# A down-projection as seven block products, with the operand sums on GpSimd

## The chip, the cores and the metric

The kernel runs on one core of one Trainium2 chip. The time is device microseconds of that core for one execution; the time before is the median of three runs. All lengths below are microseconds (us) unless ns is written. PE is the TensorE matmul engine and PEld its weight load, DVE is VectorE, ACT is ScalarE, POOL (Pool in the text) is GpSimd, SP issues DMAs, and a q behind a name is that engine's queue.

## The reference, cut to what matters

A transformer-like layer on 512 tokens with 1024 features each. It has a SwiGLU feed-forward stage, a mixer of two attention branches, and a second SwiGLU stage, and everything is float32:

```python
def swiglu(x, w1, w3, w2):
    return (jax.nn.silu(x @ w1) * (x @ w3)) @ w2

x = x + 0.5 * swiglu(rmsnorm(x, ffn1_norm[l]), ffn1_w1[l], ffn1_w3[l], ffn1_w2[l])
h = rmsnorm(x, mix_norm[l])
x = x + hybrid_mixer(h, w_in[l], b_gate[l], ...)
x = x + 0.5 * swiglu(rmsnorm(x, ffn2_norm[l]), ffn2_w1[l], ffn2_w3[l], ffn2_w2[l])
return rmsnorm(x, final_norm)
```

The inner width of a feed-forward stage is 2816, which is 22 chunks of 128. The change is in the last line but one, the second feed-forward stage (called "b" in the code): its down-projection is the product with `ffn2_w2`.

## The kernel before

Activations stand transposed: features on the 128 partitions, the 512 tokens along the free dimension. The state x is eight tiles of 128x512, `x0` to `x7` (listed as x_74 to x_81 in the order of instructions). To keep float32 accuracy with the fast matmul format, every operand is split into a high part H and a rest L, and a product is three matmuls (`mm3`, L260): H·H, H·L, L·H. A weight chunk of 128x1024 is loaded by DMA into a raw buffer, cast on ACT into `wh` (L247) and subtracted on DVE into `wl` (L248). There are four pairs of `wh` and `wl`, taken in turn, so a chunk can be cast once the chunk four places earlier has been used up on PE.

Stage b works in three groups of inner chunks, 0 to 8, 8 to 16 and 16 to 22. In each group:

- **Up.** Pairs of chunks f are computed by `strassen`: a 2x2 block product with seven block products in place of eight. Its steps are A11, S1, S2, A12, S3, S4, A22 (`STEPS`). S1 and S3 are sums of two blocks of weights, formed by a DMA that loads one block and a second DMA, issued by Pool, that adds the other on the way (L228, `wt`). S2 and S4 are sums formed on DVE (L246, `ws`). The operands on the other side are blocks of the activations; the PSUM banks called mm, X and Y collect the products, and `evict` moves them out after each step. One step is 24 matmuls of 128x256. The steps of consecutive pairs are interleaved.
- **Gate.** `evict` multiplies with the norm factor R, applies Silu, multiplies the two branches and keeps the result as H and L (`keep2`, L503 and L504) in the tiles `gg`.
- **Down.** `blocks` (L389) multiplies the group's 8 chunks with 64 blocks of `ffn2_w2`: 64 times three matmuls of 128x512, 192 in all, for the second group. Eight chunks of weights are loaded for it. Each of the eight output rows is then scaled by R and subtracted into x on DVE (L581, L582; the sign and the half are in the factor -0.5).

PE runs in an order written out by hand. The order on ACT, DVE, Pool and SP is set by a scheduler when the program is built. Each engine takes its instructions strictly in order, so an instruction that waits holds up everything behind it on its engine.

Of the kernel before, what the change touches and what calls it, by code (L numbers as in the profile page):

```python
# [30 lines left out]
GAP_S = 6  # L31
GAP_B = 1
LAG = 1
LAST = 2
WARM = 4
T = 512
# [30 lines left out]
def f32(t):  # L67
    return t.bitcast(F32)


class Layer:
# [53 lines left out]
    def turn_of(self, n):  # L125
        if self.kind[n] != "wt":
            return n
        s, f = self.order[n][0][2], self.order[n][1][0]
        if s == "q":
            return max(n - EARLY, self.index["swq", (0, "A11")] - 1)  # L130
        return n - (EARLIER if f >= GROUPS[s][1] else EARLY)
# [9 lines left out]
    def ffn_order(self, s):  # L141
        first, *ends = GROUPS[s]
        items, lo, n = [("w13" + s, i) for i in range(2 * first)], first, 0
        for hi in ends:
            items += [("sw" + s, at) for at in self.slots(range(lo, hi, 2), not lo)]
            nf = hi - (0 if n == 0 else lo)
# [35 lines left out]
    def offset(self, n):  # L182
        name, key = self.order[n][:2]
        if name[:2] == "sw":
            return 160 - 128 * (n % 2)
        if name == "w2b" and key >= (NF + GROUPS["b"][2]) // 2:
            return 96
        return 160 if name in ("w2a", "w2b", "wpa", "wpb", "wo") else 224
# [10 lines left out]
    def load(self, n):  # L199
# [16 lines left out]

        def part(q):
            if name[2] == "q" and f == FV:
                return self.a["wav0"][2 * int(q[1]) + int(q[2]) - 3].rearrange("p (a c) -> p a c", a=2)
# [11 lines left out]
    def prep(self):  # L231
# [5 lines left out]
        if both is None:  # L237
            return False
        name, key = self.order[n][:2]
        if n not in self.raws:  # L240
            self.load(n)
        raw, (H, L) = self.raws[n], both
        if name[:2] == "sw" and key[1] in ("S2", "S4"):
            a, b = (self.raws[self.index[name, (key[0], q)]] for q in (("S1", "A11") if key[1] == "S2" else ("S2", "A12")))
# [75 lines left out]
    def strassen(self, s, fs, evict):  # L320
        st, order = {}, self.slots(fs, s == "b" and not fs[0])
        end = self.used + len(order) - 1
        for f, step in order:
# [15 lines left out]
            evict(f, step, ps)  # L339
            yield  # L340

    def right(self, step, k):
# [139 lines left out]
    def ffn_run(self, s, gin, gnext, hooks, out=None, side={}):  # L482
# [33 lines left out]
        def folded(f):  # L516
            return out is not None and f >= ends[-2]

        def scale(t, a):
            t = t.rearrange("p (j n) -> p j n", j=2)  # L520
            nc.vector.tensor_mul(t, t, self.R[:, 256 * a:256 * a + 256].unsqueeze(1).to_broadcast([128, 2, 256]))

        def evict(f, step, ps):
# [15 lines left out]
            elif step == "S3":  # L539
                nc.vector.tensor_add(c2, ps, c2)  # L540
                if folded(f):
                    scale(lo, 0)
                    scale(c2, 1)
            elif step == "S4" and folded(f):
# [3 lines left out]
            elif step == "S4":  # L548
# [3 lines left out]
                nc.vector.tensor_mul(q, q, R)  # L552
                nc.scalar.activation(c1, c1, AF.Silu)
            else:
                if folded(f):
# [51 lines left out]
        for gi, hi in enumerate(ends):  # L607
# [8 lines left out]
            def done(d, ps, gi=gi, last=last):  # L616
                down(d, ps, last)
                if (gi, d) in side:
                    side[gi, d]()

            rows = [(list(g), lambda ps, d=d: done(d, ps)) for d in range(NK)]
            if last and out is not None:
# [752 lines left out]
def arrange(inp):  # L1375
# [9 lines left out]
    gqk = np.stack([p["q_norm"][0][half], p["k_norm"][0][half]]).reshape(1, 2, 2, 64)  # L1385
    out["gqk"] = np.broadcast_to(gqk, (128, 2, 2, 64))
    for s, n in (("a", 1), ("b", 2)):
        w1 = feat_chunks(p[f"ffn{n}_w1"][0])
# [5 lines left out]
        w2 = p[f"ffn{n}_w2"][0]  # L1394
        out["w2" + s] = np.concatenate([block_chunks(w2[128 * lo:128 * hi], LAST) for lo, hi in zip(ends, ends[1:])])
    w = p["w_in"][0]
# [32 lines left out]
```

## Time and profile before

| | us |
|---|---|
| median of 3 runs (lowest to highest) | 1240.81 (1240.38 to 1241.09) |
| profiled execution, its own time | 1240.7 |
| its span in the trace | 1238.9 |
| up part of the second group, stage b (1018.60 to 1094.87) | 76.27 |
| down part of it (1094.87 to 1138.41) | 43.54 |

The span is the stretch between the first and the last instruction in the trace; the profiled execution's time is 1.8 us longer. PE is busy for 99% of the span. A group of instructions is listed as line, engine, operation, out<-in; a timeline row is start, duration, engine, line, operation. PE rows overlap, since matmuls are pipelined: the pace of PE is read from the starts.

### The profile page before, as it was taken

How to read it: one execution, taken by the hardware profiler on the slowest of the kernel's cores; microseconds unless marked ns; L12 is line 12 of the kernel's file. 1: busy time of each engine (PE TensorE's matmuls, PEld its weight loads, DVE VectorE, ACT ScalarE, POOL GpSimd, SP SyncE). 2: the span in 40 equal slices, each digit the busy share in tenths (PEclk: the TensorE clock that was granted, in tenths of full speed). 3: DMA queues.
4: the chain of work that ended last, by engine and by line, in shares of the span. 5: the costliest groups of instructions: out<-in, count | busy, mean ns of one | idle time of the engine just before them, and what ended most of it. 6: DMA issues, size and time to landing. Idle time of an engine off the chain costs nothing.

```text
span 1238.9 us, 20489 instructions
## 1 busy us (share of the span) xinstructions
PE 1231.2 (99%) x8225; PEld 1115.5 (90%) x8225; DVE 906.2 (73%) x1348; ACT 605.9 (49%) x899; POOL 125.7 (10%) x131
## 2 busy tenths in 40 slices
PE   9999999999999999999999999999999999999998
PEld 7897999899899999988888888888899989988997
DVE  6985688468787887467746888865988757875874
ACT  7652355145465444454424446654665425532554
POOL 1111110000212110200001100000211001100001
PEclk9999999999999999999999999999999999999999
DMA  8783787241488972653232231267668537744222
GB/s 291 225 225 112 215 236 188 92 113 58 142 217 249 235 224 103 226 175 93 81 121 88 68 119 44 74 216 250 199 171 196 175 89 190 194 144 114 57 86 68
DMA packets 90206, 190.96 MB, mean 154 GB/s; under 512 B 12816, under 2 KB 18496, under 8 KB 90112
## 3 DMA queue, kind: packets, MB, share of 16 engines
q1 hardware_dynamic: 70896, 145.58, 34.7%
q0 software_dynamic: 18496, 43.54, 17.5%
q8 instruction: 64, 1.05, 0.3%
q10 hardware_dynamic: 720, 0.55, 0.1%
q14 instruction: 30, 0.25, 0.1%
HBM read 175.91 MB, written 17.38 MB: 156 GB/s over the span
## 4 chain that ended last, share of the span: by engine, by line
PE 98%; issue 1%; DMA 0%; SPq 0%; POOL 0%; POOLq 0%; ACT 0%; DVE 0%
PE mm L262 25%; PE mm L264 24%; PE mm L263 24%; PE Y L262 4%; PE Y L264 4%; PE Y L263 4%; PE X L262 2%; PE X L263 2%; PE X L264 2%; PE S L945 1%; PE mm L1023 1%; PE Tb L1159 1%; PE T L1034 1%; PE Sb L264 1%; PE Sb L263 1%
## 5 line engine op out<-in xcount | busy, mean ns | idle before, releaser
L247 ACT CAST wh<-wr 128x1024 fp32r<-128x1024 f32 x133 | 139.6, 1050 | 187.6 <-PE mm L263 129.5
L248 DVE TENSOR_TENSOR wl<-wr,wh 128x1024 fp32r<-128x1024 f32 x133 | 163.0, 1226 | 52.2 <-ACT wh L247 52.0
L262 PE MATMUL mm<-hH,wh 128*128 128x256 f32 (+1 forms) x560 | 179.5, 321 | 0.2 <-ACT wh L1300 0.2
L264 PE MATMUL mm<-hH,wl 128*128 128x256 f32 (+1 forms) x560 | 177.0, 316 | 0.0
L263 PE MATMUL mm<-hL,wh 128*128 128x256 f32 (+1 forms) x560 | 176.7, 316 | 0.0
L262 PE MATMUL mm<-gg,wh 128*128 128x512 f32 (+1 forms) x440 | 166.4, 378 | 0.0
L263 PE MATMUL mm<-gg,wh 128*128 128x512 f32 (+1 forms) x440 | 165.9, 377 | 0.0
L264 PE MATMUL mm<-gg,wl 128*128 128x512 f32 (+1 forms) x440 | 165.9, 377 | 0.0
L262 PEld LDWEIGHTS mm<-hH,wh 128*128 128x128 f32 x560 | 105.2, 188 | 9.2 <-ACT wh L1300 1.0
L264 PEld LDWEIGHTS mm<-hH,wl 128*128 128x128 f32 x560 | 105.1, 188 | 8.3 <-DVE wl L1301 0.4
L263 PEld LDWEIGHTS mm<-hL,wh 128*128 128x128 f32 x560 | 105.3, 188 | 7.4 <-DVE hL L411 0.2
L247 ACT CAST wh<-wa 128x1024 fp32r<-128x1024 f32 x54 | 56.8, 1051 | 94.6 <-PE mm L263 47.0
L262 PEld LDWEIGHTS mm<-gg,wh 128*128 128x128 f32 x440 | 82.6, 188 | 15.5 <-PE mm L264 0.2
L264 PEld LDWEIGHTS mm<-gg,wl 128*128 128x128 f32 x440 | 82.6, 188 | 15.4
L263 PEld LDWEIGHTS mm<-gg,wh 128*128 128x128 f32 x440 | 82.6, 188 | 15.0
L247 ACT CAST wh<-ws 128x1024 fp32r<-128x1024 f32 x54 | 56.8, 1052 | 71.3 <-PE mm L263 49.3
L247 ACT CAST wh<-wt 128x1024 fp32r<-128x1024 f32 x54 | 56.8, 1052 | 64.9 <-PE mm L263 41.6
L262 PE MATMUL mm<-TH,wh 128*128 128x256 f32 x320 | 88.4, 276 | 0.0
L263 PE MATMUL mm<-TL,wh 128*128 128x256 f32 x320 | 88.3, 276 | 0.0
L264 PE MATMUL mm<-TH,wl 128*128 128x256 f32 x320 | 88.3, 276 | 0.0
L248 DVE TENSOR_TENSOR wl<-wt,wh 128x1024 fp32r<-128x1024 f32 x54 | 65.9, 1223 | 28.6 <-ACT wh L247 27.9
L248 DVE TENSOR_TENSOR wl<-wa,wh 128x1024 fp32r<-128x1024 f32 x54 | 65.9, 1220 | 22.9 <-ACT wh L247 22.9
(284 smaller groups left out, 3198.5 us busy)
## 6 DMA issues: line engine op xcount, KB each, us to landing
wr<-in_w2a SPq DMA_DIRECT2D x22, 512.0 KB, 3.8
wt<-in_w13b SPq DMA_DIRECT2D x22, 512.0 KB, 3.8
wa<-in_w13b SPq DMA_DIRECT2D x22, 512.0 KB, 3.4
wt<-in_w13b POOLq DMA_DIRECT2D x22, 512.0 KB, 5.9
wr<-in_w2b SPq DMA_DIRECT2D x22, 512.0 KB, 3.7
wt<-in_w13a SPq DMA_DIRECT2D x18, 512.0 KB, 5.7
wt<-in_w13a POOLq DMA_DIRECT2D x18, 512.0 KB, 7.0
wa<-in_w13a SPq DMA_DIRECT2D x18, 512.0 KB, 6.5
```

The lines of the kernel that those rows point to most:

```text
L247: self.nc.scalar.copy(H, raw)
L248: self.nc.vector.tensor_sub(L, raw, f32(H))
L262: mm(out, lH, rH, start=start, stop=False, skip_group_check=more)
L263: mm(out, lH, rL, start=False, stop=False, skip_group_check=more)
L264: mm(out, lL, rH, start=False, stop=stop, skip_group_check=more)
L945: nc.tensor.matmul(*args, start=True, stop=True)
L1023: nc.tensor.matmul(oc, v, p, start=st, stop=sp)
L1034: nc.tensor.transpose(ps[:, 128 * b:128 * b + 128], P[h][:, c0 + 128 * b:c0 + 128 * b + 128], self.ident)
L1159: nc.tensor.transpose(pt[:, 128 * j:128 * j + 128], P[h, j][:, 128 * k:128 * k + 128], self.ident)
```

## The change

For the second group of stage b (`DOWN = (('b', 1),)`) the down-projection becomes a 2x2 block product too. The inner width of 1024 is split into two halves of 512, the 1024 outputs into two halves of 512 and the tokens into two halves of 256. The 512 outputs of a half are worked in two pieces of 256 (`half` 0 and 1). Each of the seven steps is done for both pieces: 14 products of 24 matmuls of 128x256, so 336 matmuls instead of 192 of 128x512. A11 is issued in two parts: three of its four chunks of the inner width for both pieces, then the fourth for both, which comes from the last pair of the up part.

Weights: `w2d` holds four blocks for each piece. S1 and S3 come by two DMAs as in the up part, S2 and S4 are sums on Pool (new L256). So 14 chunks are cast and split instead of 8, and 12 loads of 512 KB replace 8.

Activations: the gated result is kept as float32 in four blocks b0 to b3 (`G["t"]`, listed as T-2 and T-1) instead of being split. The seven operands are b0, b0-b1, -(b3+b0-b1), b2, b3-b1, b3 and (b3+b0-b1)-b2. The sums run on Pool in place (new L584, L586, L595, L600), and each operand is then cast on ACT and split on DVE (`divide`, new L575, L576, L578, L579) into two alternating buffers.

Scaling: R is applied in the up part's eviction for this group, the second scaling of each branch on Pool (new L628). Results: A11, S1 and S2 leave PSUM by an ACT copy and are added to x on Pool in pieces of 128x256 (new L613, L615). A12, S3, S4 and A22 are added to x on DVE straight from PSUM (new L619).

```diff
+DOWN = (('b', 1),)
...
+        if name[3:] == "d" and key[1] in ("S2", "S4"):
+            a, b = (self.raws[self.index[name, (key[0], q)]] for q in (("S1", "A11") if key[1] == "S2" else ("S2", "A12")))
+            self.nc.gpsimd.tensor_add(raw, a, b)
...
+    def down2(self, s, at, parts, evict):
+        name, st = "sw" + s + "d", {}
+
+        def products(half, step, cur, ops, ks=range(4)):
+            bank = {"S1": "Y", "S4": "Y", "A12": "X"}.get(step, "A")
+            fresh = step in ("A11", "S1", "A12") and 0 in ks
+            if fresh:
+                st[half, bank] = self.bank() if bank == "A" else self.aux(bank)
+            ps = st[half, bank]
+            for j in range(2):
+                for k in ks:
+                    w = [t[:, 512 * j + 128 * k:512 * j + 128 * k + 128] for t in cur]
+                    self.mm3(ps[:, 256 * j:256 * j + 256], *w, *(t[:, k] for t in ops), fresh and j == 0 and k == 0, k == 3,
+                             not (step in ("A11", "S1", "A12") and j == 0))
+            if 3 in ks:
+                evict(half, step, ps)
+
+        cur = [self.weights(name, ((at, half), "A11")) for half in range(2)]
+        ops = parts[0]()
+        for ks in (range(3), range(3, 4)):
+            for half in range(2):
+                products(half, "A11", cur[half], ops, ks)
+        ops = [parts[1]()]
+        for i, step in enumerate(STEPS[1:], 1):
+            ops.append(parts[i + 1]() if i < 6 else None)
+            for half in range(2):
+                products(half, step, self.weights(name, ((at, half), step)), ops[i - 1])
...
+        def divide(step, src, ks, sign=1.0):
+            H, L = (t[:, ks] for t in block(step))
+            if sign > 0:
+                nc.scalar.copy(H, src[:, ks])
+                nc.vector.tensor_sub(L, src[:, ks], f32(H))
+            else:
+                nc.scalar.activation(H, src[:, ks], AF.Copy, scale=sign)
+                nc.vector.scalar_tensor_tensor(L, src[:, ks], sign, f32(H), op0=ALU.mult, op1=ALU.subtract)
+
+        def first_parts(ks):
+            b = G["b"]
+            divide("A11", b[0], ks)
+            nc.gpsimd.tensor_sub(b[0][:, ks], b[0][:, ks], b[1][:, ks])
+            divide("S1", b[0], ks)
+            nc.gpsimd.tensor_add(b[0][:, ks], b[3][:, ks], b[0][:, ks])
...
+                if step in ("A11", "S1", "S2"):
+                    u = self.tmp.tile([128, T], F32, tag="t", name="u")
+                    nc.scalar.activation(u, ps, AF.Copy, scale=sign)
+                    for j, d in enumerate(rows):
+                        nc.gpsimd.tensor_add(self.x[d][:, cs], self.x[d][:, cs], u[:, 256 * j:256 * j + 256])
+                    return
+                for j, d in enumerate(rows):
+                    x = self.x[d][:, cs]
+                    self.pin = nc.vector.scalar_tensor_tensor(x, ps[:, 256 * j:256 * j + 256], sign, x, op0=ALU.mult, op1=ALU.add)
```

How the instructions stand at two places. The first is the passage from the up part of the second group to its down part. DVE, before (wl are the rests of weight chunks, c the gate's tiles, gg the split result, u and x the output):

```order
L552 TENSOR_TENSOR c_10998<-c_10998,R 128x1024
L248 TENSOR_TENSOR wl<-wr,wh 128x1024
L557 TENSOR_TENSOR c_10998<-mm,c_10998 128x512
L559 TENSOR_TENSOR c_10998<-c_10998,c_10999 128x512
L248 TENSOR_TENSOR wl<-wr,wh 128x1024
L504 TENSOR_TENSOR gg<-c_10998,gg 128x2x2x256
L248 TENSOR_TENSOR wl<-wr,wh 128x1024
L581 TENSOR_TENSOR u<-mm,R 128x512
```

DVE, after the change, at the same place:

```order
L628 TENSOR_TENSOR c_11010<-c_11010,R 128x512
L262 TENSOR_TENSOR wl<-wt,wh 128x1024
L668 TENSOR_TENSOR T-1_10706<-c_11010,c_11011 128x2x256
L669 TENSOR_TENSOR T-2_10705<-mm,c_11010 128x2x256
L262 TENSOR_TENSOR wl<-wt,wh 128x1024
L576 TENSOR_TENSOR gg<-T-2_10705,gg 128x256 x2
L262 TENSOR_TENSOR wl<-ws,wh 128x1024
L579 SCALAR_TENSOR_TENSOR gg<-T-2_10705,gg 128x1024
L262 TENSOR_TENSOR wl<-ws,wh 128x1024
L262 TENSOR_TENSOR wl<-wa,wh 128x1024 x2
L576 TENSOR_TENSOR gg<-T-2_10705,gg 128x1024
```

The two gate products (L668, L669) stand between weight splits, and the last pieces of the operands A11 and S1 (the two of 128x256), then those of S2 and A12, behind them. On Pool the before has only DMA issues here; with the change there stands:

```order
L256 TENSOR_TENSOR ws<-wt,wa 128x1024
L237 DMA wt<-in_w2d 128x1024
L584 TENSOR_TENSOR T-2_10705<-T-2_10705,T-1_10706 128x768
L628 TENSOR_TENSOR c_11010<-c_11010,R 128x512
L586 TENSOR_TENSOR T-2_10705<-T-1_10706,T-2_10705 128x768
L628 TENSOR_TENSOR c_11011<-c_11011,R 128x512
L584 TENSOR_TENSOR T-2_10705<-T-2_10705,T-1_10706 128x256
L595 TENSOR_TENSOR T-1_10706<-T-1_10706 128x1024
L586 TENSOR_TENSOR T-2_10705<-T-1_10706,T-2_10705 128x256
```

The sum for S3 (L595) was moved by the scheduler ahead of the last piece of the sum for S2 (L586). The second place is the middle of the down part, steps S2 to A22. Pool:

```order
L256 TENSOR_TENSOR ws<-ws,wa 128x1024
L615 TENSOR_TENSOR x_78<-x_78,u 128x256
L615 TENSOR_TENSOR x_79<-x_79,u 128x256
L256 TENSOR_TENSOR ws<-ws,wa 128x1024
L615 TENSOR_TENSOR x_80<-x_80,u 128x256
L615 TENSOR_TENSOR x_81<-x_81,u 128x256
L600 TENSOR_TENSOR T-2_10705<-T-2_10705 128x1024
L615 TENSOR_TENSOR x_74<-x_74,u 128x256
```

And DVE, from the split of S3's operand to that of A22's:

```order
L576 TENSOR_TENSOR gg<-T-1_10706,gg 128x1024
L619 SCALAR_TENSOR_TENSOR x_74<-X,x_74 128x256
L619 SCALAR_TENSOR_TENSOR x_75<-X,x_75 128x256
L262 TENSOR_TENSOR wl<-ws,wh 128x1024
L260 TENSOR_TENSOR ws<-wt,wa 128x1024
L619 SCALAR_TENSOR_TENSOR x_76<-X,x_76 128x256
L619 SCALAR_TENSOR_TENSOR x_77<-X,x_77 128x256
L262 TENSOR_TENSOR wl<-ws,wh 128x1024
L576 TENSOR_TENSOR gg<-T-1_10706,gg 128x1024
```

Four weight sums and splits, one weight sum for the next group (L260) and the results of A12 stand ahead of the operand of S4 (the last row). Before the change nothing of these was there but weight splits and the pairs L581 and L582.

More of the change, by code (lines that the diff above doesn't have):

```diff
@@ L145, in ffn_order @@
             items += [("sw" + s, at) for at in self.slots(range(lo, hi, 2), not lo)]
-            nf = hi - (0 if n == 0 else lo)
+            nf = hi - (0 if lo == first else lo)
+            if (s, ends.index(hi)) in DOWN:
+                at = DOWN.index((s, ends.index(hi)))
+                items += [("sw" + s + "d", ((at, half), step)) for step in STEPS for half in range(2)]
+                nf = 0
             items += [("w2" + s, n + i) for i in range(nf)]
@@ L516, in folded, with paired, block @@
         def folded(f):
-            return out is not None and f >= ends[-2]
-        def scale(t, a):
+            return out is not None and f >= ends[-2] or paired(f)
+        def paired(f):
+            return (s, sum(f >= e for e in ends)) in DOWN
+        G, ring = {}, {}
+        def block(step):
+            if step not in ring:
+                t = self.gtile(2 + STEPS.index(step) % 2)
+                ring[step] = [t[:, 1024 * c:1024 * c + 1024].rearrange("p (k n) -> p k n", k=4) for c in range(2)]
+            return ring[step]
@@ new lines, in evict2, with fn @@
+        def evict2(gi):
+            calls = iter(range(NK))
+            def fn(half, step, ps):
+                rows = range(2 * half, 2 * half + 2) if step in ("A11", "S2", "A12", "S4") else range(2 * half + 4, 2 * half + 6)
+                sign = -0.5 if rows[0] < 4 else 0.5
+                cs = slice(256, 512) if step in ("S1", "S2", "S3", "S4") else slice(0, 256)
+                if step in ("A11", "S1", "S2"):
[7 more added lines that the diff above has]
+                    self.pin = nc.vector.scalar_tensor_tensor(x, ps[:, 256 * j:256 * j + 256], sign, x, op0=ALU.mult, op1=ALU.add)
+                d = next(calls)
+                if (gi, d) in side:
+                    side[gi, d]()
+            return fn
@@ L1386, in arrange @@
     out["gqk"] = np.broadcast_to(gqk, (128, 2, 2, 64))
+    pairs = {}
     for s, n in (("a", 1), ("b", 2)):
@@ L1394, in arrange @@
         w2 = p[f"ffn{n}_w2"][0]
-        out["w2" + s] = np.concatenate([block_chunks(w2[128 * lo:128 * hi], LAST) for lo, hi in zip(ends, ends[1:])])
+        spans = list(zip(ends, ends[1:]))
+        out["w2" + s] = np.concatenate([block_chunks(w2[128 * lo:128 * hi], LAST) for i, (lo, hi) in enumerate(spans)
+                                        if (s, i) not in DOWN])
+        for at, (st, i) in enumerate(DOWN):
+            if st == s:
+                lo, hi = spans[i]
+                b = w2[128 * lo:128 * hi].reshape(4, 2, 128, 2, 2, 2, 128)
+                pairs[at] = b.transpose(4, 3, 1, 2, 5, 0, 6).reshape(2, 4, 128, 1024)
+    out["w2d"] = np.stack([pairs[at] for at in range(len(DOWN))])
     w = p["w_in"][0]
```

50 lines of the change are left out of this document (44 added, 6 removed).

## The prediction

> **What bounds the kernel now.** I read the page's busy times and its chain of waits first, then the stretches around the changed place.
>
> ```profile
> span 1238.9 us, 20489 instructions
> ...
> PE 1231.2 (99%) x8225; PEld 1115.5 (90%) x8225; DVE 906.2 (73%) x1348; ACT 605.9 (49%) x899; POOL 125.7 (10%) x131
> ...
> PE 98%; issue 1%; DMA 0%; SPq 0%; POOL 0%; POOLq 0%; ACT 0%; DVE 0%
> ```
>
> The chain is 98% PE: time changes one for one with what PE issues, as long as it does not wait. By stretch (columns: PE, PEld, DVE, ACT, Pool busy with counts, clock, DMA), the second group's up part and its down part:
>
> ```profile
> core 0: us, PE busy (x) PEld busy (x) DVE busy (x) ACT busy (x) POOL busy (x), PEclk, DMA share, GB/s
> 1018.60:1094.87 76.27, 76.27 (x674) 76.27 (x672) 62.35 (x62) 41.68 (x47) 8.44 (x7) 1.00 0.72 188
> 1094.87:1138.41 43.54, 43.54 (x194) 36.04 (x193) 23.10 (x27) 9.90 (x11) 1.20 (x1) 1.00 0.35 107
> ```
>
> PE never waits in either. DVE is 82% busy in the up part and 53% in the down part, ACT 55% and 23%, and Pool does nothing but issue DMAs. So the down part has much cover, and Pool looks free. The pace, from the starts of matmuls in time order:
>
> ```profile
> 1089.43 0.28 PE L262 MATMUL Y<-hH,wh 128*128 128x256 f32 x1
> ...
> 1092.15 0.28 PE L262 MATMUL mm<-TH,wh 128*128 128x256 f32 x1
> ...
> 1094.87 0.39 PE L262 MATMUL mm<-gg,wh 128*128 128x512 f32 x1
> ...
> 1138.41 0.28 PE L262 MATMUL mm<-hH,wh 128*128 128x256 f32 x1
> ...
> 1217.76 0.28 PE L263 MATMUL mm<-gg,wh 128*128 128x256 f32 x1
> ...
> 1221.64 0.28 PE L263 MATMUL mm<-gg,wh 128*128 128x256 f32 x1
> ```
>
> **Removed and added on PE.** Before: 192 matmuls in 43.54. After: 336 of 128x256, and 24 of those take 2.72 in a step of the up part, so 38.08: a gain of 5.46. The last two rows (33 matmuls in 3.88, 0.118 each) would make it 39.5 and the gain 4.0. I take 2.72, the same kind of step with the same weight loads. This gain holds only if 14 weight chunks and seven operands arrive in time.
>
> **What the operands cost.** The prices, from groups and single rows:
>
> ```profile
> L247 ACT CAST wh<-wr 128x1024 fp32r<-128x1024 f32 x133 | 139.6, 1050 | 187.6 <-PE mm L263 129.5
> L248 DVE TENSOR_TENSOR wl<-wr,wh 128x1024 fp32r<-128x1024 f32 x133 | 163.0, 1226 | 52.2 <-ACT wh L247 52.0
> ...
> L644 POOL TENSOR_TENSOR x<-x,R 128x256 f32<-128x256 f32 x2 | 1.4, 724 | 9.5 <-ACT R L454 9.5
> ...
> L228 POOL DMA_DIRECT2D wt<-in_w13b x22 | 26.6, 1232 | 395.5 <-DMA wt<-in_w13b 185.3 <-DVE u L581 93.7 <-DVE c L535 59.4
> ...
> 1085.65 0.68 DVE L557 TENSOR_TENSOR c<-mm,c 128x512 f32<-128x512 f32 x1
> ...
> 1214.30 0.42 DVE L578 SCALAR_TENSOR_TENSOR x<-mm,x 128x256 f32<-128x256 f32 x1 [1.43 <-PE mm L264]
> ```
>
> By these alone DVE has in the down part 14 splits of 1.23, about six operand splits of 1.23 and 16 evictions of 0.42, 31 of 38, and everything fits. But Pool's sums and DVE's splits do not run side by side. The places in the trace where both worked, DVE first:
>
> ```profile
> 868.49 0.42 DVE L894 TENSOR_TENSOR Traw<-Traw 128x256 f32<-128x256 f32 x1
> ...
> 873.50 1.25 DVE L894 TENSOR_TENSOR Traw<-Traw 128x256 f32<-128x256 f32 x1 [0.19 <-ACT Traw L890]
> ...
> 875.27 1.21 DVE L248 TENSOR_TENSOR wl<-wr,wh 128x1024 fp32r<-128x1024 f32 x1
> 876.40 0.47 DVE L411 SCALAR_TENSOR_TENSOR hL<-x,par,hH 128x256 fp32r<-128x256 f32 x1
> 876.80 0.67 DVE L1271 TENSOR_TENSOR x<-x,mm 128x512 f32<-128x512 f32 x1
> 877.40 1.88 DVE L248 TENSOR_TENSOR wl<-wr,wh 128x1024 fp32r<-128x1024 f32 x1
> 879.20 1.51 DVE L411 SCALAR_TENSOR_TENSOR hL<-x,par,hH 128x256 fp32r<-128x256 f32 x1
> ```
>
> ```profile
> 872.94 1.52 POOL L421 TENSOR_TENSOR acc<-acc,sq 128x512 f32<-128x512 f32 x1 [4.09 <-ACT sq L419]
> 874.41 2.44 POOL L228 DMA_DIRECT2D wt<-in_w13b  x2
> 876.57 1.61 POOL L421 TENSOR_TENSOR acc<-acc,sq 128x512 f32<-128x512 f32 x1
> 878.68 1.74 POOL L421 TENSOR_TENSOR acc<-acc,sq 128x512 f32<-128x512 f32 x1 [0.50 <-ACT sq L419]
> ...
> 1206.07 1.29 POOL L421 TENSOR_TENSOR acc<-acc,sq 128x512 f32<-128x512 f32 x1 [54.56 <-ACT sq L419]
> ```
>
> A Pool sum alone takes 1.29; beside DVE 1.52 to 1.74. The DVE instructions with two inputs in SBUF that start inside a Pool sum grow from 0.42 to 1.25, 1.21 to 1.88, 0.47 to 1.51. Taken off the recorded ends, each began 0.12 to 0.18 before the other's end: the two take turns, whoever asked first. An instruction with one input in PSUM (L1271, 0.67) is not held, nor is anything by a DMA issue (874.41). So a Pool sum of 512 holds DVE for 1.14 (from 878.07 to 879.13 the DVE split held Pool 1.06, from 879.13 to 880.24 Pool held DVE 1.11, and the one before 1.18). From the two sizes, 0.72 and 1.29, a quarter more of width is 0.57: holds of 0.57, 1.14, 1.71 and 2.28 for 256, 512, 768 and 1024. A DVE split holds Pool 1.07, one of 768 0.8, of 512 0.53, of 256 0.27.
>
> **The sum of the turns.** Zero is the end of the up part on PE. The last stretch without slack begins at -11.1: the second weight sum for S2 on Pool needs a buffer that DVE releases at -11.2 (its weight pair is free at -13.6, then 1.05 on ACT and 1.23 on DVE). From there to the split of A22's operand the order holds on Pool 5 sums of 1024, 2 of 768, 2 of 512 and 10 of 256: 11.4 + 3.4 + 2.3 + 5.7 = 22.8. On DVE 21 of 1024, 2 of 768, 3 of 512 and 2 of 256: 22.5 + 1.6 + 1.6 + 0.5 = 26.2. Together 49.0, so A22 cannot start before 37.9; without waits it would at 32.64 (12 of 14 products). At least 5.3 is lost of 5.46, with no pause in the turns. That is the bound from below. The bound from above is no waiting at all.
>
> **A walk through the order** with these holds, casts of 1.05 (0.35 for 256) and PE at 2.72 a product gives the pauses. The second weight sum ends at -8.8, a DMA issue follows to -7.5, the difference b0-b1 (three chunks) waits for its split at -6.85 and ends at -5.05. DVE's scaling is held until then; Pool's scale of the Silu branch runs to -2.2, DVE's split of S1's operand to -1.35, Pool's sum b0 to 0.4, the weight split of A11's second piece to 1.5, Pool's second scale to 2.6. Then in line on DVE: scaling 3.2, split 4.3, gate products 4.9 and 5.5, split 6.6, and the last chunk's split 6.95. PE wants it at 4.08: **a wait of 2.9**. The last chunk of S1 stands behind the sum for S3, moved ahead of it (7.7 to 9.95): **0.9**. S2 is on time (operand at 14.15, wanted at 14.67). Behind it four weight splits and four pieces of x alternate, and A12's operand comes at 20.2, **0.1** late. Pool's first sum for S4 follows (21.85 to 24.1), a split (25.2), a piece of x (25.75) and the operand of S3 at 26.85, wanted at 25.65: **1.2**. Then a piece of x to 27.4, DVE's two evictions of A12 to 27.6, and here Pool's second sum for S4 (27.55) and DVE's next split (27.6) ask within 0.1 of each other. If Pool is first: its sum to 29.8, split 30.9, piece 31.45, weight sum for the third group 32.55, evictions and the sum b2 to 35.5, split 36.6, piece 37.15, operand of S4 at 38.25, wanted at 32.3. If DVE is first, b2 falls behind that operand, which is there at 35.6: **6.0 or 3.3**. A22 then has its operand in time, and behind it the third group's first weights, four pairs ahead, are not late. Together 8.4 to 11.1, less 5.46: 3.0 to 5.6 slower. I take the middle, 4.3. On the profiled execution's 1240.7, which is 0.1 under the median, that is 1245.
>
> [...]
>
> The other edits change nothing on the path. Four more loads of 512 KB in the down part come at the up part's cadence, where DMA is busy 72% and PE doesn't wait. In the up part DVE loses a Silu scaling of 1024 and a split per pair and gains scalings; Pool's two scalings of 1.14 per pair take turns within DVE's 18% of slack, up to -11.
>
> **Rivals.**
> - *Clean gain.* Pool's turns are absorbed, since chunks can be cast three products (8.2) ahead and ACT is half idle. Then the gain is 4.0 to 5.46, less perhaps a wait of 1: 1235.3 to 1238. For it: PE has no wait in either part now. Against it: the 49.0 of turns in 43.7 (from -11.1 to 32.64). 17%.
> - *About nothing.* The turns interlock without pause, or Pool's pieces of x come late and out of the way: lost 5.3, gained 5.46, or with the last four pieces of x counted too (2.3) 2.1 slower: 1240.5 to 1243. 13%.
> - *Worse than the walk.* PE stands for 3.3 to 6.0 at S4 and comes back slower. The one slow stretch of this trace is its start:
>
> ```profile
> 4.83 0.79 PE L262 MATMUL mm<-hH,wh 128*128 128x512 f32 x1
> 5.42 0.48 PE L263 MATMUL mm<-hL,wh 128*128 128x512 f32 x1
> 5.74 0.41 PE L264 MATMUL mm<-hH,wl 128*128 128x512 f32 x1
> ...
> 7.15 0.39 PE L264 MATMUL mm<-hH,wl 128*128 128x512 f32 x1
> ```
>
> The first two come after 0.59 and 0.32 instead of 0.23, some 0.45 lost. Against that low price stands that PE had been at work before. At half pace for one product, 2.72 more, on the walk's upper end of 1246.3: 1249; the same after the wait at A11: 1252. 15%. [...]
> - *The change does not do what it says:* PE runs 128x256 at no better than 0.118: inside the first rival.
>
> **How the numbers follow.** The walk has 55%, with 1243.3 to 1249 as its own range. 0.2%, 2.5, is what a measurement here can tell from no change. Slower by more is the walk and the worse case, 70%; within it 13%; faster 17%. The range that leaves out some 10% of the clean gain below and some 8% above is 1236.5 to 1252.
>
> **What would show it.** Right: PE waits in the changed part, the first of 2 to 4 at A11's fourth chunk, the longest at S4, released by DVE's L576; DVE splits of 1.9 to 3.5 beside Pool sums of 1024; the down part 46 to 50 long. Wrong: a down part of 38 to 40 with splits of 1.23, or sums on Pool of 2.4 with unheld splits beside them. If instead PE waits for `wt` or `wr` DMAs, the loads were underrated. If the up part grows beyond 76.3, the scalings were.

## The result and the profile after

The changed kernel takes 1252.59 us (median of 4 runs, 1251.64 to 1253.83); the kernel before took 1240.95 beside it (4 runs). The ratio is 1.0095, with a 95% interval of 1.0078 to 1.0113: slower by 11.6, where the forecast was 4.3 slower and a range to 1252.0. The direction was right, the size was not. The profiled execution took 1253.83 and has a span of 1252.1.

The head of the page and its chain of waits, after the change. PE is still busy for 98% of a longer span, but DVE and Pool now stand in the chain:

```profile
span 1252.1 us, 20884 instructions
...
PE 94%; DVE 2%; issue 2%; POOL 1%; DMA 0%; ACT 0%; SPq 0%; POOLq 0%; DVEq 0%
```

By stretch (columns: PE, PEld, DVE, ACT, Pool busy with counts, clock, DMA, GB/s): the up part to its last matmul ahead of a pause, then that pause to the first matmul of the down part, then the down part:

```profile
1018.18:1092.30 74.12, 74.12 (x652) 74.00 (x650) 66.02 (x57) 38.50 (x47) 24.28 (x16) 1.00 0.69 178
1092.30:1099.53 7.23, 4.31 (x28) 4.14 (x27) 7.20 (x7) 2.17 (x4) 5.32 (x3) 0.82 0.42 132
1099.53:1151.74 52.21, 43.25 (x338) 42.66 (x337) 48.70 (x41) 23.40 (x28) 29.98 (x22) 0.89 0.56 145
```

The up part and the pause are 81.35 against 76.27, the down part is 52.21 against 43.54 (38.08 if nothing waited). Two of the three clocks are below 1.00. PE's waits in this stretch (us in total, times, longest), and the matmuls on both sides of each pause:

```profile
PE X L277 <- DVE gg L576: 6.7, 1, 6.7
PE mm L276 <- DVE c L647: 2.9, 1, 2.9
PE mm L277 <- DVE gg L576: 2.1, 1, 2.1
```

```profile
1092.30 0.28 PE L278 MATMUL Y<-hH,wl 128*128 128x256 f32 x1
1095.50 0.36 PE L276 MATMUL mm<-TH,wh 128*128 128x256 f32 x1 [2.92 <-DVE c L647]
...
1117.02 0.28 PE L276 MATMUL X<-gg,wh 128*128 128x256 f32 x1
...
1124.01 0.58 PE L277 MATMUL X<-gg,wh 128*128 128x256 f32 x1 [6.72 <-DVE gg L576]
...
1131.22 0.28 PE L276 MATMUL mm<-gg,wh 128*128 128x256 f32 x1
...
1133.60 0.38 PE L277 MATMUL mm<-gg,wh 128*128 128x256 f32 x1 [2.11 <-DVE gg L576]
```

The first pause lies in the up part, at the last step of its last pair; the second is at A12's operand, the third at S3's. None is at A11's fourth chunk or at S4.

**A ledger.** From the starts of all matmuls between 1018 and 1160 I count each gap above 0.3, less the 0.113 of a matmul at full pace (2.72 / 24), as a pause, and each gap of 0.14 to 0.3, less 0.113, as lost pace. After the change the pauses come to 12.8 and the lost pace to 5.4; less the 5.46 that PE gains this is 12.7, and the two spans differ by 13.2. The same count is made for the kernels below and comes within 0.9 of the spans. The parts are:

| | pause | lost pace behind it |
|---|---|---|
| up part, bank read by L647 (1092.30 to 1095.50) | 3.1 | 1.6 |
| S1, small (1106.47 to 1106.88) | 0.3 | |
| A12 (1117.02 to 1124.01, with 0.3 behind it) | 7.1 | 1.6 |
| S3 (1131.22 to 1133.60) | 2.3 | 1.6 |

The three stretches at half pace, 16 matmuls each, make 4.8 of the 5.4; the rest are single gaps, in some of which a record may be missing.

**The lost pace** is the granted clock. The stretch of matmuls at half pace that ends at 1100.38 is 3.41 long; in stretches of that length, counted from its end:

```profile
1093.55:1096.97 3.42, 1.47 (x12) 1.50 (x13) 3.42 (x3) 0.85 (x1) 2.52 (x3) 1.00 0.48 153
1096.97:1100.38 3.41, 3.41 (x18) 3.41 (x17) 3.38 (x4) 0.92 (x2) 1.91 (x1) 0.50 0.42 135
...
1127.68:1131.10 3.42, 3.42 (x31) 3.42 (x31) 3.42 (x2) 1.05 (x1) 3.42 (x4) 1.00 0.02 5
1131.10:1134.50 3.40, 1.29 (x11) 1.09 (x10) 3.40 (x5) 1.99 (x2) 0.23 (x1) 1.00 0.62 199
1134.50:1137.92 3.42, 3.42 (x19) 3.42 (x18) 3.38 (x5) 0.01 (x1) 1.50 (x2) 0.51 0.69 146
```

The two stretches in which PE works 1.47 of 3.42 and 1.29 of 3.40 are each followed by one whole stretch at 0.50 or 0.51, with 18 or 19 matmuls instead of 31. The stretch ahead of the first of them, 1090.14 to 1093.55, in which PE works 2.43 of 3.41, is followed by one at 1.00. The stretches at half pace behind the three pauses end on one grid of 3.41: at 1100.38, at 1127.7 (8 times 3.41 later) and at 1137.9 (11 times).

**What held DVE.** In the up part Pool's difference b0-b1 (L584) and its scaling (L628) hold two DVE instructions, and L647, which frees the bank that PE waits for, stands behind them. First Pool, then DVE:

```profile
1089.27 1.85 POOL L584 TENSOR_TENSOR T-2_10705<-T-2_10705,T-1_10706 128x768 f32<-128x768 f32 x1 [1.30 <-DVE gg L576]
...
1092.66 1.27 POOL L628 TENSOR_TENSOR c<-c,R 128x512 f32<-128x512 f32 x1 [1.54 <-ACT c L645]
```

```profile
1089.75 1.92 DVE L628 TENSOR_TENSOR c<-c,R 128x512 f32<-128x512 f32 x1
...
1092.73 2.02 DVE L576 TENSOR_TENSOR gg<-T-2_10705,gg 128x768 fp32r<-128x768 f32 x1
1094.67 0.68 DVE L647 TENSOR_TENSOR c<-mm,c 128x512 f32<-128x512 f32 x1
```

At A12 the turns that the forecast relied on are not kept. DVE, then Pool:

```profile
1111.15 1.76 DVE L262 TENSOR_TENSOR wl<-ws,wh 128x1024 fp32r<-128x1024 f32 x1
...
1114.51 4.80 DVE L262 TENSOR_TENSOR wl<-wa,wh 128x1024 fp32r<-128x1024 f32 x1
1119.24 4.72 DVE L576 TENSOR_TENSOR gg<-T-2_10705,gg 128x1024 fp32r<-128x1024 f32 x1
1123.88 6.86 DVE L262 TENSOR_TENSOR wl<-wt,wh 128x1024 fp32r<-128x1024 f32 x1
```

```profile
1115.15 0.73 POOL L615 TENSOR_TENSOR x<-x,u 128x256 f32<-128x256 f32 x1
1115.84 2.37 POOL L256 TENSOR_TENSOR ws<-ws,wa 128x1024 f32<-128x1024 f32 x1
1118.18 1.71 POOL L615 TENSOR_TENSOR x<-x,u 128x256 f32<-128x256 f32 x1
1119.86 0.71 POOL L615 TENSOR_TENSOR x<-x,u 128x256 f32<-128x256 f32 x1
1120.54 2.33 POOL L256 TENSOR_TENSOR ws<-ws,wa 128x1024 f32<-128x1024 f32 x1
```

The split at 1114.51 asks while a Pool sum runs that ends at 1115.18. Strict turns would start it there. Instead the next sum (0.73, its length alone) and a weight sum (2.37) go first, and only the third is held (1.71). The same happens to A12's operand (4.72), and at 1123.88 five sums pass a split. Against turns of 1.74 the two instructions ahead of A12 lose 3.1 and 3.0: most of the pause of 7.0.

### The profile page after: what moved, and what is told of

Its sections match the earlier page's. It is cut to its first block, busy times and chain, and to the rows that moved or that the text cites. A ratio compares the mean times of both kernels' runs of the same rounds, so it can differ in the third digit from the quotient of the medians.

```text
span 1252.1 us, 20884 instructions
## 1 busy us (share of the span) xinstructions
PE 1232.4 (98%) x8369; PEld 1123.3 (90%) x8369; DVE 943.0 (75%) x1363; ACT 619.0 (49%) x920; POOL 176.7 (14%) x165
## 4 chain that ended last, share of the span: by engine, by line
PE 94%; DVE 2%; issue 2%; POOL 1%; DMA 0%; ACT 0%; SPq 0%; POOLq 0%; DVEq 0%
PE mm L276 23%; PE mm L278 23%; PE mm L277 23%; PE Y L276 4%; PE Y L278 4%; PE Y L277 4%; PE X L276 2%; PE X L278 2%; PE X L277 2%; PE S L1068 1%; DVE wl L262 1%; PE mm L1146 1%; PE Tb L1282 1%; PE T L1157 1%; DVE gg L576 1%
## 5 line engine op out<-in xcount | busy, mean ns | idle before, releaser
L261 ACT CAST wh<-wr 128x1024 fp32r<-128x1024 f32 x127 | 133.3, 1050 | 173.8 <-PE mm L277 115.0
L262 DVE TENSOR_TENSOR wl<-wr,wh 128x1024 fp32r<-128x1024 f32 x127 | 159.2, 1253 | 50.9 <-ACT wh L261 50.8
L277 PE MATMUL mm<-gg,wh 128*128 128x512 f32 (+1 forms) x440 | 159.7, 363 | 2.1 <-DVE gg L576 2.1
L276 PE MATMUL mm<-gg,wh 128*128 128x512 f32 (+1 forms) x440 | 160.3, 364 | 0.0
L278 PE MATMUL mm<-gg,wl 128*128 128x512 f32 (+1 forms) x440 | 159.7, 363 | 0.0
L261 ACT CAST wh<-wa 128x1024 fp32r<-128x1024 f32 x58 | 60.9, 1051 | 89.5 <-PE Y L277 46.6
L261 ACT CAST wh<-ws 128x1024 fp32r<-128x1024 f32 x58 | 61.0, 1051 | 78.7 <-PE mm L277 43.7
L262 DVE TENSOR_TENSOR wl<-wt,wh 128x1024 fp32r<-128x1024 f32 x58 | 76.9, 1329 | 27.5 <-ACT wh L261 27.0
L278 PEld LDWEIGHTS mm<-gg,wl 128*128 128x128 f32 x440 | 83.5, 190 | 12.7
L262 DVE TENSOR_TENSOR wl<-wa,wh 128x1024 fp32r<-128x1024 f32 x58 | 79.4, 1370 | 19.1 <-ACT wh L261 19.1
L261 ACT CAST wh<-wt 128x1024 fp32r<-128x1024 f32 x58 | 60.9, 1051 | 63.1 <-PE mm L277 38.4
```

What stands on the lines that cost most here:

```text
L261: self.nc.scalar.copy(H, raw)
L262: self.nc.vector.tensor_sub(L, raw, f32(H))
L276: mm(out, lH, rH, start=start, stop=False, skip_group_check=more)
L277: mm(out, lH, rL, start=False, stop=False, skip_group_check=more)
L278: mm(out, lL, rH, start=False, stop=stop, skip_group_check=more)
```

## The experiments

The kernel before was timed beside all runs; its medians lie between 1240.66 and 1240.95. The ratios below are to it.

### Is it Pool's reads?

The first run takes the 12 sums of results on Pool away: A11, S1 and S2 are added to x by DVE, straight from PSUM.

```diff
-                if step in ("A11", "S1", "S2"):
-                    u = self.tmp.tile([128, T], F32, tag="t", name="u")
-                    nc.scalar.activation(u, ps, AF.Copy, scale=sign)
-                    for j, d in enumerate(rows):
-                        nc.gpsimd.tensor_add(self.x[d][:, cs], self.x[d][:, cs], u[:, 256 * j:256 * j + 256])
-                    return
...
+                if step in ("A11", "S1", "S2"):
+                    return
```

The loop between these lines, which adds A12, S3, S4 and A22 to x on DVE, now serves all steps.

> The results of A11, S1 and S2 are added to x on DVE straight from PSUM (one input in PSUM, 0.42 each), instead of an ACT copy and twelve Pool sums of 128x256; all else as in the change. Theory P (Pool's sums keep DVE's two-input instructions off SBUF, and do so for several sums in a row): the twelve sums are most of Pool's unbroken stretch of 1110 to 1131, so the wait of 6.9 at A12 falls to 2 or less and that of 2.3 at S3 with it; 1242 to 1247. Rival Q (Pool is only too slow, and DVE waits for its results): A12's operand b2 needs no sum, so its wait stays at 6 to 7; 1250 to 1253. Rival R (DVE has too much work): 12 instructions of 0.42 more on DVE, 1253 to 1257.

The second leaves every Pool sum out and lets Pool write the same output three times with memsets, which read nothing.

```diff
-            self.nc.gpsimd.tensor_add(raw, a, b)
+            self.fill(raw)
```

`fill` writes three memsets; all other Pool sums are replaced likewise, so the output is another one.

> Every sum that the change put on Pool is left out and three memsets of the same output stand in its place, so Pool is busy about as long and writes the same places, but reads nothing; the result is another one. Theory P: without reads DVE isn't held, the splits are back at 1.22, no wait at A12 or S3; 1235 to 1239. Rival Q (Pool's length and order alone are late): the waits stay; 1248 to 1254.

Measured: 1246.82 (1246.52 to 1247.34; ratio 1.0049, 1.0033 to 1.0066) and 1238.51 (1237.83 to 1238.99; ratio 0.9981, 0.9970 to 0.9991). Of PE's waits, in the first those in the up part and at A12, in the second the longest:

```profile
PE mm L276 <- DVE c L643: 2.9, 1, 2.9
...
PE X L277 <- DVE gg L576: 0.2, 1, 0.2
```

```profile
PE mm L277 <- DVE gg L583: 0.9, 1, 0.9
```

Without the 12 sums the wait at A12 is 0.2 instead of 6.7 and the one at S3 0.7 instead of 2.1, the one of 2.9 in the up part stays, and a new one of 1.9 stands at S2. With memsets in place of all sums the longest wait is 0.9 and the pauses come to 2.1; beside the memsets around the passage to the down part DVE's splits take 1.22. But this run does not tell reads from time at A12: a memset waits for no input, so the 36 memsets of x ran from 986.7 to 1021.5, some 90 or more ahead of their place, and behind 1114.4 Pool only issues DMAs. That a Pool sum holds DVE and a memset of the same width does not (3.36 and 1.21 beside 128x1024) is shown by the next kernel.

### The price of a turn

A measuring kernel of its own, which leaves the layer out: DVE differences of 128x1024 beside Pool sums of three widths, beside memsets, and with DVE's first input in PSUM; then matmuls with pauses of PE between them.

> A kernel of its own that leaves the layer out and only measures: 14 DVE differences of 128x1024 (two SBUF inputs) beside a full queue of Pool sums of 256, of 512 and of 1024, beside Pool sums that each wait for an ACT copy, beside Pool memsets, and 14 with one input in PSUM beside Pool sums of 1024; then matmuls after pauses of PE of about 1 to 6 us. Turn by turn (the prediction's rule): a DVE instruction takes 1.7 beside sums of 256, 2.3 beside 512, 3.4 beside 1024; Pool's sums grow by 1.07 each. If Pool keeps its place while its queue is full: single DVE instructions wait for 4 and more sums, others go two or three in a row. Memsets and the PSUM input: 1.14 to 1.22. PE: full pace after pauses up to about 3, half pace for some 3 us after longer ones, if the pause is the cause.

Rows of DVE, two in succession beside 256, one beside 1024, and one with its input in PSUM:

```profile
37.19 1.74 DVE L51 TENSOR_TENSOR owith<-xa,pb 128x1024 f32<-128x1024 f32 x1
38.86 1.74 DVE L51 TENSOR_TENSOR owith<-xa,pb 128x1024 f32<-128x1024 f32 x1
...
106.04 3.36 DVE L51 TENSOR_TENSOR owith<-xa,pb 128x1024 f32<-128x1024 f32 x1
...
198.30 1.22 DVE L51 TENSOR_TENSOR opsum<-wide,pb 128x1024 f32<-128x1024 f32 x1
```

Here the turns are strict, 1.74 for each DVE instruction beside 256, 2.28 beside 512, 3.36 beside 1024 (1.21 alone): each sum of a quarter more width adds 0.54, where the forecast had 0.57. Beside memsets and with an input in PSUM DVE takes 1.21 and 1.22. So the prices of the forecast were right, and the long rows of the changed kernel need something that this kernel does not have.

The matmuls show the clock again. Behind a pause of 2.7 (217.56 to 220.25) a stretch at about half pace follows at once; behind one of 3.3 PE runs 1.06 at full pace and then a stretch at half:

```profile
220.25:223.60 3.35, 3.35 (x16) 3.35 (x17) 0.00 (x0) 0.00 (x0) 0.00 (x0) 0.51 0.00 0
...
244.06:247.45 3.39, 3.39 (x18) 3.39 (x17) 0.00 (x0) 0.00 (x0) 0.00 (x0) 0.50 0.00 0
```

The ends, 223.6 and 247.45, are 7 times 3.41 apart, though the pauses differ (2.7 and 3.3). The expectation had full pace after pauses of up to about 3, a limit that no run shows; that failed, as the half pace behind 2.7 says.

### Is it the clock?

14 matmuls on R ahead of A12, which are overwritten, keep PE busy while it waits for A12's operand; nothing else is changed.

```diff
+            for _ in range({("A12", 0): 14}.get((step, half), 0) if fresh else 0):
+                self.nc.tensor.matmul(ps[:, :256], self.R[:, :128], self.R[:, :256], start=True, stop=True)
```

> Fourteen matmuls of R with itself (128x256, float32, into the bank that A12 overwrites) are put ahead of A12, into the wait of 6.9; their product is used by nothing. Theory: the half pace behind the pauses (0.21 per matmul, 3.4 us lost in the down part) comes of PE's standing still; kept busy, it loses 1.4 to 3.4 less: 1249 to 1251. Rival: the pace falls for another reason (power, the operands): 1252 to 1254, no gain.

Measured: 1253.51 (1252.92 to 1254.84; ratio 1.0104, 1.0089 to 1.0119), no gain: the time of the rival, though not for its reason. The stretch behind A12, and the one behind S3:

```profile
1123.04:1126.00 2.96, 2.96 (x25) 2.96 (x26) 2.96 (x1) 0.02 (x1) 2.96 (x3) 1.00 0.49 176
...
1132.65:1137.00 4.35, 4.35 (x20) 4.35 (x21) 4.32 (x7) 0.00 (x0) 1.89 (x2) 0.50 0.71 169
```

The half pace behind A12 is gone, so it did come of PE's standing still. But S3's operand comes no earlier for it (16.6 after the start of the pause at A12 in both kernels): PE waits 3.9 there instead of 2.3, and pays the clock behind that, for more than one stretch of 3.41 (4.35 at 0.50). The 1.6 that the dummies saved at A12 is waited at S3. Where a row of late operands sets the time, a faster PE between two of them is worth nothing.

### Moving the sums to DVE, part by part

Scalings alone (L628), results and scalings, these and the weight sums (L256), and all, with the operand sums (L584, L586, L595, L600); then the operand sums alone, and all but the results. The results go to DVE as in the first run; each other part is the same edit at its line:

```diff
-            self.nc.gpsimd.tensor_add(raw, a, b)
+            self.nc.vector.tensor_add(raw, a, b)
```

Where these expectations and the later ones speak of a port, the rows show that DVE and Pool take turns (1.74 beside sums of 256) and that memsets have no part in it (1.21), and no more than that.

> One part of the change alone is undone: the two scalings per pair of the gate that ran on Pool (L628) run on DVE again; all other Pool sums stay. Theory P (DVE stands behind Pool's sums at the shared port): PE's pause of 3.2 in the up part, at the bank that L647 reads, came from DVE instructions held by these scalings, each 1.14. With them gone the pause is under 1, the half pace after it (2.0) goes too, and the time is 5.2 below the changed kernel's 1252.6: 1246 to 1249, with the pause of 7.0 at A12 still there. Rival Q (the pause comes from Pool's weight sum for S2 and from b0-b1, not from the scalings): the pause stays between 2 and 4 and the time at 1251 to 1254.

> Results of A11, S1 and S2 on DVE from PSUM (as in x_on_dve) and also the scalings on DVE. Pool keeps four weight sums and six operand sums. Theory P: the up part's pause of 3.1 and the half pace after it go, 5 less than x_on_dve's 1246.8: 1240.5 to 1243.5, what is left being pauses of 1 to 2 in S2 and S3. Rival Q (another sum sets the up part's pause): 1246 to 1248. Rival D (DVE's own work becomes the bound: two scalings of 0.67 per pair and 12 evictions of 0.42 are 7 more on DVE): pauses released by DVE grow in the down part, 1244 to 1247 with no pause in the up part.

> As the one before, and the weight sums for S2 and S4 on DVE too. Pool keeps only the six operand sums. DVE gets four sums of 1.23 (4.9) and loses four holds of 2.28 (9.1). Theory P: 1237 to 1240, with pauses of under 2 in all. Rival D (DVE's work is the bound): about the same as with the weight sums on Pool, 1240.5 to 1243.5.

> Every sum of the change on DVE, Pool only issues DMAs. Theory P: no hold is left; DVE has 21 splits of 1.23, 5 sums of 1.23, some 7 of smaller size and 24 evictions of 0.42 in the last 49 before A22, some 45, so it fits only just, and pauses of 1 to 3 stay: 1236 to 1240, the gain of 5.5 less the pauses. Rival D (DVE's own time is what the change costs wherever the sums run): 1241 to 1246.

> Only the operand sums (L584, L586, L595, L600) move to DVE; scalings, weight sums and x sums stay on Pool. Adding up what each part was worth when it was moved (6.9 for the operand sums, as the last part moved): 1245 to 1247. If the parts are not to be added because one row of Pool sums is as good as another at passing DVE over: the pause at A12 stays at 3 to 7 and the time at 1249 to 1253.

> Pool keeps only the 12 sums per half-group of results into x (24 of 256, 0.57 of hold each) with their ACT copies; scalings, weight sums and operand sums run on DVE. Against every sum on DVE (1237.4) DVE saves the evictions of A11, S1 and S2, 12 of 0.42, 5.0, and is held 12 times 0.57, 6.8. Theory A (strict turns): within 2 of 1237.4, 1236 to 1240. Theory B (Pool's row of sums passes DVE over for several sums at a time): single DVE instructions of 3 to 7, a PE pause of 2 to 5 with half pace after it, 1240 to 1245.

(There are 12 sums of 256 for the results, not 24.) Measured, with the ledger's two sums:

| on DVE | median | ratio, 95% interval | pauses | lost pace |
|---|---|---|---|---|
| nothing (the change) | 1252.59 | 1.0095 (1.0078 to 1.0113) | 12.8 | 5.4 |
| results | 1246.82 | 1.0049 (1.0033 to 1.0066) | 7.1 | 4.1 |
| scalings | 1252.90 | 1.0096 (1.0081 to 1.0112) | 12.8 | 4.7 |
| results, scalings | 1248.45 | 1.0062 (1.0049 to 1.0074) | 8.9 | 3.4 |
| results, scalings, weight sums | 1244.28 | 1.0028 (1.0017 to 1.0039) | 5.7 | 2.3 |
| operand sums | 1247.55 | 1.0055 (1.0040 to 1.0070) | 7.7 | 4.0 |
| all but the results | 1243.86 | 1.0023 (1.0013 to 1.0033) | 6.0 | 3.1 |
| all | 1237.37 | 0.9973 (0.9963 to 0.9982) | 1.2 | 0.4 |

With all sums on DVE the change is 0.27% faster than the kernel before: 3.4 of the 5.46 arrive, and one wait of 0.8 is left. This version beats both kernels, though DVE has the most instructions there (1393 against 1363 in the changed kernel): its busy time even falls, from 943.0 to 928.3, since nothing holds it (splits of 1.21 and 1.22 at the passage to the down part).

The expectation for the scalings was wrong. The pause in the up part did fall from 3.1 to 1.3, so they made the larger half of it, but DVE's own work then comes later into the down part: PE waits 3.6 at S1 and 4.3 at S2, no longer at A12, and the time stays. Also with the results already on DVE, moving the scalings costs 1.6. The parts do not add up: the results are worth 5.8 as the first part to go and 6.5 as the last, the operand sums 5.0 and 6.9, the scalings nothing or less. What a sum costs depends on what it stands in front of. Of the other expectations here, those for all sums on DVE (theory P) and for all but the results (theory B) held; results with scalings (1248.45) and these with the weight sums (1244.28) came out above all their windows, and the operand sums alone (1247.55) between their two.

### When does Pool pass DVE over?

A second measuring kernel: the sums in place, mixed widths, DVE starting at other moments, and DMA issues of Pool directly ahead of its sums.

> A measuring kernel of its own that leaves the layer out: 12 to 14 DVE differences of 128x1024 beside a row of Pool sums, in sections: DVE's first start shifted by 0.2 to 0.7 (four sections), Pool's 24 sums of 256 in place, a mix of 256, 256 and 1024 in place, two accumulating DMA issues or two plain ones directly ahead of the 24 sums with DVE starting at once or 1.4 later, and a mix in which each two sums wait for a fresh ACT copy, without and with the accumulating issues ahead. Theory A (strict turns everywhere, DVE was not ready in the changed kernel for another reason): every DVE instruction that meets 256-wide sums takes 1.74, and none waits for more than one sum. Theory M (an issue of a DMA on Pool leaves its sums overlapping, so that the port does not come free between them): waits over several sums, 2.4 and more, in the sections with an issue ahead and in no other. Theory I (sums in place keep the port): in the in-place sections too. Theory O (it depends on when DVE asks): in some of the shifted sections, with nothing else changed.

In the four shifted sections, with sums in place, with the mix, and with sums that wait for ACT, the turns are strict throughout (1.74, and 3.35 beside 1024). Behind two DMA issues they are not (the issue, the first DVE row that meets the sums, and Pool's 24 sums as one row):

```profile
195.56 1.19 POOL L90 DMA_DIRECT2D acc<-in_x  x1
196.13 16.86 POOL L83 TENSOR_TENSOR x<-x,u 128x256 f32<-128x256 f32 x24
```

```profile
195.91 18.17 DVE L46 TENSOR_TENSOR odma<-xa,pb 128x1024 f32<-128x1024 f32 x1
```

One DVE instruction waits for the whole row of 24 sums, 18.17 instead of 1.74; 17.55 and 17.40 behind plain loads. With the accumulating issues and DVE asking later it is passed over in no place, and in the mix behind an issue only by the sums of 1024, 4.04 instead of 3.35. So in this kernel no DVE instruction is passed over without an issue ahead, as theory M said, and an issue does not always suffice. A third kernel asks what ends it.

> A second measuring kernel that leaves the layer out: what ends the row in which Pool's sums pass DVE over after Pool has issued DMAs. Sections, each with 8 DVE differences of 128x1024: two plain issues, then 16 sums of 256 with a Pool memset of 64, 256 or 512 between them (the memset does not use the port); one memset of 512 only between the issues and the sums; a wait of Pool for eight ACT copies there; the issues in the middle of a row of 18; accumulating issues with DVE asking 0.7 to 2.8 later; sums of 1024 behind issues. If Pool's sums pass DVE over because the next one asks before the last one has let go everywhere (the start of one overlaps the end of the one before), a memset between them lets DVE in: no DVE instruction above 2 in the sections with memsets between, and above 5 in the section with none. If it is a state that an issue leaves for a length of time (the descriptors are still being worked on), the section with the wait shows turns of 1.74 and the memsets change nothing. In the middle of a row: 1.74 ahead of the issues, passed over behind them.

A row of 16 sums directly behind two plain issues passes DVE over (12.19); one memset of 0.54 in between restores the turns (1.74). Each time DVE, then Pool:

```profile
300.36 12.19 DVE L46 TENSOR_TENSOR oagain<-xa,pb 128x1024 f32<-128x1024 f32 x1
...
85.18 1.74 DVE L46 TENSOR_TENSOR oonce<-xa,pb 128x1024 f32<-128x1024 f32 x1
```

```profile
300.55 10.91 POOL L83 TENSOR_TENSOR x<-x,u 128x256 f32<-128x256 f32 x16
...
84.16 0.54 POOL L92 MEMSET gap<- 128x512 f32 x1
```

Memsets of 256 or 512 between the sums restore the turns too, those of 64 do not (13.53), and a wait of Pool for ACT does. With the issues in the middle of a row the turns hold ahead of them, and behind them DVE waits 9.4 for the twelve sums that are left. When DVE asks later behind accumulating issues, two of four sections are passed over (12.17, 12.12) and two are not: it depends on the moment as well. Behind issues, rows of six sums of 1024 pass DVE over too (14.99 and 15.77). Neither theory fits whole: by the first the memsets of 64 should have let DVE in, by the second no memset should have, and no row shows the descriptors that it speaks of.

### Does passing over make the loss?

Every sum stays on Pool; behind each of the down part (not behind the scalings) comes a memset on a tile that is free there, and behind the accumulating loads of stage b from its second group on one of 128x512 (the first run has both, the second only the latter, the third both on the version with only the results on Pool).

```diff
+    def gap(self, inst, w):
+        with self.tc.issue_after(inst.ins):
+            self.nc.gpsimd.memset(self.acc[:, :w], 0.0)
...
-            self.nc.gpsimd.tensor_add(raw, a, b)
+            self.gap(self.nc.gpsimd.tensor_add(raw, a, b), 256)
```

> The changed kernel with a Pool memset of 128x256 on a free tile behind each Pool sum of the down part, and one of 128x512 behind each of Pool's accumulating loads. Nothing is left out and no sum is moved from Pool; Pool's row gets about 5 longer. In the measuring kernel such memsets gave the port to DVE after each sum. Theory B (being passed over by several sums in a row makes the pause of 7.0 at A12 and the 2.4 at S3): no DVE instruction in the down part above 3.5, the pause at A12 under 2, the time 1246 to 1250, near the 1245 that strict turns gave on paper plus the 5 of the up part's pause. Theory A (the sum of the turns sets the time, and who goes first only moves the waits): the pauses of the down part come to 8 to 12 again, later ones in place of the one at A12, and the time is 1250.5 to 1255.

> Only the memsets of 128x512 behind Pool's accumulating loads, none between the sums. Theory B1 (an issue of a DMA puts Pool in the state in which its sums pass DVE over, and one memset of 0.5 ends that state): as with all the memsets, 1246 to 1250. Theory B2 (once in the state, only a memset between the sums themselves lets DVE in, or the memset is not directly behind the issue): DVE instructions of 4 and more stay, the time 1250 to 1254.

> Pool keeps only the 12 sums of results into x, each followed by a memset of 128x256, and the memsets of 512 behind the loads; scalings, weight sums and operand sums run on DVE. Without the memsets this was 1243.9, with one DVE instruction of 4.1, a pause of 4.6 at S2 and half pace of 3.1 in all. Theory B: these go and the time is 1237 to 1239.5. Theory A: the pause moves and stays above 3, 1241.5 to 1244.5.

Measured: 1249.93 (1249.55 to 1250.49; ratio 1.0074, 1.0060 to 1.0087), 1254.08 (1253.26 to 1254.60; ratio 1.0108, 1.0093 to 1.0124) and 1246.61 (1244.02 to 1247.15; ratio 1.0041, 1.0029 to 1.0054). In the first the passing over is gone, A12's operand is held by one sum, and PE doesn't wait for it; but it waits 5.4 at S4's operand (and 1.1 at S1's, which stands in the same row of the waits):

```profile
1115.35 1.76 DVE L582 TENSOR_TENSOR gg<-T-2_10712,gg 128x1024 fp32r<-128x1024 f32 x1
```

```profile
PE Y L283 <- DVE gg L582: 6.5, 2, 5.4
PE mm L282 <- DVE c L653: 3.1, 1, 3.1
```

The pauses come to 11.9 against 12.8, the lost pace to 1.9 against 5.4. Theory A is right on the pauses: 8.5 of the pauses lie in the down part, most at S4, the place and about the size that the walk of the prediction gave (6.0). The time is 2.7 lower, inside B's window at its upper end, and most of that is the clock: behind the pause of 3.3 in the up part PE runs at full clock (1.00 from 1095.30 to 1098.70), and no stretch at half pace follows those of 0.6 and 1.2 either.

In the second the rows of 4 and more stay (8.85 and 6.83 on DVE), as B2 said, at the upper edge of its window. It does not settle whether an issue is the trigger in the changed kernel, since the second of the two memsets was scheduled four sums behind its load. In the third neither theory held: it is slower than without the memsets. There a split is passed over by four sums although a memset stands behind each:

```profile
1110.16 5.52 DVE L268 TENSOR_TENSOR wl<-wa,wh 128x1024 fp32r<-128x1024 f32 x1
```

```profile
1109.35 1.20 POOL L241 DMA_DIRECT2D wt<-in_w13b  x1
...
1110.60 1.19 POOL L621 TENSOR_TENSOR x<-x,u 128x256 f32<-128x256 f32 x1
1111.28 0.76 POOL L208 MEMSET acc<- 128x256 f32 x1
```

Behind this accumulating load Pool's rows overlap by about 0.5 (a sum runs from 1110.60 to 1111.79, the memset from 1111.28), longer than the memset of 0.3 itself takes. A pause on Pool shorter than that overlap lets nobody in; that is an inference from these rows. What makes the rows overlap, and why in the changed kernel DVE is passed over at some sums with an overlap of only 0.04 (0.73 from 1115.15, and the next at 1115.84), stays open.

## Why the prediction was right and wrong

- **The gain on PE, 5.46, was right.** With it the ledger closes within 0.9 for every kernel: all sums on DVE loses 1.2 + 0.4, so the span should be 3.9 shorter, and it is (1235.0 against 1238.9).
- **The holds were right to a tenth of their size**: 0.57 to 2.28 per sum were forecast, and the measuring kernel shows 0.53 to 2.15 (1.74 and 3.36 less 1.21); an input in PSUM is not held (1.22), nor is DVE beside memsets (1.21). The rows of DVE beside sums of 256 start 1.67 apart (37.19 and 38.86), less than the 1.21 of the one and the 0.73 of the other alone together.
- **"The two take turns, whoever asked first" was the step that failed on the places.** It was read from three alternating pairs in the trace of before. In the changed kernel DVE is passed over by two to five sums, so the 0.1 at A12 became 7.0, and the 3.3 to 6.0 at S4 became nothing. With the turns enforced by memsets the wait is at S4, as walked.
- **The sum of the pauses in the down part came out inside nevertheless, which may be luck**: 8.4 to 11.1 were forecast and 9.7 measured, but the 2.9 at A11 and the 3.3 to 6.0 at S4 are not in it, and 7.1 at A12 is. Two other orders of the same sums give 8.5 (memsets behind all) and 10.4 (behind the loads alone), so the sum of the turns may set it; that is argued, not shown. The forecast's bound for A22's operand did not bind: its split ends at 1144.27, and PE first reads the operand at 1146.30.
- **"In the up part Pool's scalings take turns within DVE's slack" failed.** The walk itself let DVE's split of S1's operand end at -1.35, with L647 (0.68) behind it, and PE's last step of the last pair needs that bank from -2.72: 2.05 late on its own figures. I had listed the deadlines of operands and chunks and forgotten the eviction that frees a bank. Measured: a pause of 3.1. The prediction's own sign for this step came, an up part beyond 76.3: 81.35. The forecast 2.9 at A11's fourth chunk did not come, presumably since PE was already late by then.
- **The clock was the mis-sized term.** The forecast put it at nothing. "Comes back slower" had 15% as a rival, with the prices 2.72 and twice that, to 1252; it happened three times, at about 1.6 each, and the lost pace came to 5.4. The term in it, one product at half pace for 2.72 more, is shown by no run; the runs showed a stretch of 3.41 at half clock, 1.6 more. I held the start of the trace, 0.45 lost, against it; what is lost there says little about a pause between. Pauses of 12.8 and lost pace of 5.4 against the forecast's 9.75 and nothing are 8.5 more; the profiled execution lies 8.8 above the forecast. In the changed kernel the half clock followed stretches of the grid of 3.41 in which PE was idle for 1.95 and 2.11 (the second with the pause of 2.3 at S3), and not the one in which it was idle for 0.98; where the limit lies between these is not shown.
- **The other edits** cost nothing, as said: no wait of PE for `wt` or `wr` loads appears.

## What to carry to other kernels

Before work is moved to an idle Pool, ask what DVE does with two inputs in SBUF meanwhile: in the measuring kernels each Pool sum held it, for 0.53 (256 wide) to 2.15 (1024), and behind a DMA issue of Pool a whole row of 24 did, for 17. Here the same sums cost less on the busier DVE (1237.4) than on the idle Pool (1252.6). List every event that PE waits for, evictions that free a bank included, and price a pause of 2 to 3 us as the pause plus, where the grid lies so, the 1.6 us that a stretch at half clock cost here (behind pauses of 2.3 and 3.1).

## What was not expected of the hardware

- A DVE instruction with two SBUF inputs waited 18.17 for 24 Pool sums of 256 that stood directly behind Pool's DMA issues; with one memset of 0.54 behind plain issues it waited for one sum, 1.74.
- A pause of PE of 2.3 (at S3 in the changed kernel) or 2.7 (in the measuring kernel) was followed by a stretch of 3.41 or 3.35 at half clock, some 1.6 lost, and one of 3.3 by full clock (in the version with memsets behind all sums, 1.00 from 1095.30 to 1098.70). In the changed kernel it went with a grid of 3.41: behind stretches of it in which PE worked 1.47 and 1.29 the clock was half, behind one in which it worked 2.43 it was full.
